# Thirty-two bytes of padding ahead of the activation and weight pools

## The chip, the cores and the metric

The kernel runs on one core of a Trainium2 chip. The metric is device microseconds of one execution; lower is better. Three runs of the kernel before took 594.8, 599.28 and 600.5 us, so the median is 599.28 us and the runs lie 1% apart.

## The reference

A decoder trunk of two layers works on 256 tokens of width 1024, in float32. Layer 0 is causal attention (one block of 256 keys, so the block selection never selects a past block), layer 1 is attention over a window of 128 keys with sinks and keys and values shared by four query heads. Behind each attention stands a gated feed-forward part with a causal convolution of width 3. Cut to the parts that take the time:

```python
x = x + o.transpose(0, 2, 1, 3).reshape(B_, S_, N_HEADS * HEAD_DIM) @ w_o
x = x + conv_ffn(rmsnorm(x, ffn_norm[l]), w_up[l], conv_w[l], conv_b[l], w_down[l])
...
def conv_ffn(h, w_up, conv_w, conv_b, w_down):     # w_up 1024 x 5632, w_down 2816 x 1024
    u = h @ w_up
    up = jnp.pad(u, ((0, 0), (CONV_W - 1, 0), (0, 0)))
    u = conv_b + sum(conv_w[j] * up[:, j:j + S_] for j in range(CONV_W))
    gate, val = jnp.split(u, 2, axis=-1)
    return (jax.nn.silu(gate) * val) @ w_down
```

## The kernel before, in words

**Products in three.** Each float32 operand is split into a high part and a low part of type fp32r, and each product is three matmuls: high by high, high by low, low by high. The weights arrive as units of 128 partitions x 2048 numbers, 1 MB each. SyncE issues their loads into three `wr` buffers, ScalarE copies a unit to its high part `wh` (line 150), VectorE subtracts to get the low part `wl` (line 153); there are four buffers of each.

**Stages.** Layer 0: projections to q, k and v (`proj`, lines 281 to 283: 512 columns of a weight unit are the moving operand, 128 tokens of an activation tile the stationary one), attention (lines 365 to 441), output projection (`Down.mm`, lines 487, 488 and 492, in the same form), up projection (lines 575 to 577: here 256 tokens of an activation tile are the moving operand and 128 columns of a weight unit the stationary one; 22 units of 48 matmuls), down projection (`Down.mm` again). Layer 1 repeats these with narrower key and value projections.

**Order.** The order of TensorE, ScalarE and VectorE is that of emission, which `tick`, `chain` and `require` set by estimated times in the program. Nothing in these estimates looks at an address.

**Where tiles lie.** SBUF is filled pool by pool, in the order in which the pools are made, and tile by tile within a pool, each at a multiple of 32 bytes:

```python
one = ctx.enter_context(tc.tile_pool(name="one", bufs=1))
qd = ctx.enter_context(tc.tile_pool(name="qd", bufs=15))
wk = ctx.enter_context(tc.tile_pool(name="wk", bufs=2))
wp = ctx.enter_context(tc.tile_pool(name="wp", bufs=4))
```

`one` holds what stays (the residual `xr`, the identity, the values `v`, the zero-padded keys `kd`, small tables), `qd` the 15 activation tiles `q` of 4096 bytes per partition, `wk` short-lived tiles (`m2`, `m3`), `wp` the buffers `wr`, `wh` and `wl` of 8192 bytes. The places within 256 bytes, as the built program has them, since sizes in `qd` and `wp` are multiples of 256 and so every buffer of a kind has the same place:

| tiles | before | after |
|---|---|---|
| `ones`; `xr` | 0; 32 | 0; 32 |
| `ident`, `v`, `kd`, `rb` | 32, 64, 192, 0 | 64, 96, 224, 32 |
| `q` (activations, high and low) | 32 | 64 |
| `m2`, `m3` | 160, 96 | 192, 128 |
| `wr`, `wh`, `wl` (weights) | 96 | 128 |

Of the kernel before, what the change touches and what calls it, by code (L numbers as in the profile page):

```python
# [7 lines left out]
F32 = mybir.dt.float32  # L8
# [6 lines left out]
P = 128  # L15
# [22 lines left out]

# columns of the packed per-partition constants
G_ATTN0, G_KV, G_ATTN1 = 0, 8, 16  # L40
# [3 lines left out]

# weight units, in the order of their use
U_V0 = 0
# [14 lines left out]
def trunk(ctx: ExitStack, tc, x, xT, pos, cpk, fin, sinks, w, out):  # L61
# [33 lines left out]

# [1 line left out]
    # Instructions are issued in the order of emission. clock is the tensor engine's progress; what waits for another  # L97
    # engine is put off by an estimated latency, behind work that is ready by then.
    clock = [0.0]
# [17 lines left out]
    def chain(key, *steps, urgent=0):  # L117
        """steps: (delay after the step before, function)."""
        def run(k):
            if urgent:  # L120
                with tc.high_priority(offset=urgent):
                    steps[k][1]()
            else:
                steps[k][1]()
            if k + 1 < len(steps):
                put_off.append((clock[0] + steps[k + 1][0], key, lambda: run(k + 1)))
        put_off.append((clock[0] + steps[0][0], key, lambda: run(0)))

    def require(*key):
        """emit now what is put off under this key."""  # L130
        while True:
            mine = [t for t in put_off if t[1] == key]
            if not mine:
                return
            run_item(min(mine, key=lambda t: t[0]))

# [1 line left out]
    wq = {}  # L138
# [20 lines left out]
    def prepare(i):  # L159
        """split the weights of unit i, paced by the tensor engine."""  # L160
        if i >= N_UNITS:
            return
        n = 4 if i <= 5 or 1 <= i - U_UP0 <= 3 or 1 <= i - U_UP1 <= 3 else 2
        cut = [slice(k * UNIT // n, (k + 1) * UNIT // n) for k in range(n)]
        w_time[0] = max(clock[0] + 200.0, w_time[0] + 4500.0)

        def first():
            weights(i)
            hi_part(i, cut[0])

        def last():
            lo_part(i, cut[-1])
            fetch(i + 3)

        steps = [(w_time[0] - clock[0], first)]
        for k in range(n - 1):
            steps.append((2000.0 / n, lambda k=k: lo_part(i, cut[k])))
            steps.append((2000.0 / n, lambda k=k: hi_part(i, cut[k + 1])))
        chain(("w", i), *steps, (2000.0 / n, last))

    def used(i):
        """all products with unit i are emitted: its place is that of unit i + 4."""
        prepare(i + 4)
# [13 lines left out]

# [1 line left out]
    ident = one.tile([P, P], F32, name="ident")  # L199
# [10 lines left out]
    def warm_up(n):  # L210
        """products that nothing reads keep the tensor engine's clock up while the first loads are under way."""
        if n:
            t = bank("u")
            for _ in range(int(n)):
                nc.tensor.matmul(t[:, :P], ones, ones, start=True, stop=True)

# [1 line left out]
    sums = {}  # L218

    def new_hT():  # L220
        """feature-major activations: hi and lo, 8 chunks of [128, 256] in two tiles each."""
        return [(quad(), quad()) for _ in range(2)]

    def feats(b, n, sets, key, keep=None):
        """half n of the residual of token block b, times gains, to feature-major hi and lo parts."""
        ts = [bank("t"), bank("t")]
        for j in range(4):
            nc.tensor.transpose(ts[j // 2][:, (j % 2) * P:(j % 2 + 1) * P],
                                xr[b][:, (4 * n + j) * P:(4 * n + j + 1) * P], ident)
        tick(450)  # L230

        def steps(hT, g, y, m):
            c = slice(2 * m, 2 * m + 2)
            hi, lo = (part[:, c, blk(b)] for part in hT[n])
            y_ = y[:, c]

            def gain():
                for j in range(2):
                    col = g + 4 * n + 2 * m + j
                    nc.scalar.activation(y_[:, j], ts[m][:, j * P:(j + 1) * P], AF.Copy, scale=cp[:, col:col + 1])  # L240

            def parts():
                nc.vector.tensor_copy(hi, y_)
                nc.vector.tensor_tensor(out=lo, in0=y_, in1=f(hi), op=ALU.subtract)

            return gain, parts

        for k, (hT, g) in enumerate(sets):
            y = mid().rearrange("p (j t) -> p j t", j=4) if keep is None else keep[n][:, :, blk(b)]
            for m in range(2):  # L250
                gain, parts = steps(hT, g, y, m)
                chain(key, (200.0 + 1000.0 * k + 500.0 * m, gain), (500.0, parts))
# [7 lines left out]
    def rstd_of(b):  # L260
        """rsqrt(mean(x^2) + eps) of the residual rows of token block b."""
        require("sq", b)
# [11 lines left out]
    def proj(o, hT, b, wv, units=()):  # L274
        """o[128 tokens of block b, n] = h @ W; wv(c) -> (hi, lo) of rows chunk c; units end with this block."""
        n = o.shape[-1]
# [28 lines left out]
    def rope(t, nh, b):  # L305
        """t: [128, nh, 64] in place."""
        ta = wk.tile([P, 8, ROT], F32, tag="ta", name=nm("ta"), bufs=1)[:, :nh]
# [10 lines left out]
    def to_feature(t, n, b, hi, lo, key, then=None):  # L318
        """t: [128 tokens, n*128] -> hi, lo [128, n, tokens of block b]."""
        pt = bank("t")  # L320
# [14 lines left out]
    def rotate(o, n, b, hi, lo, key, copy, then=None):  # L335
        """projection o of token block b: copy(t) scales it out of PSUM, then rope and transpose to hi, lo."""
        t = mid()[:, :n * P]
# [4 lines left out]
    def attention(qk, ready, filler, lead, rate, msk, vcol, sink):  # L342
        """8 pairs of heads; qk[g] = (q hi, q lo, k hi, k lo, k chunk, diagonal k); filler: products that fill the waits."""
        oT = []
# [89 lines left out]
        def values(j, pT):  # L434
            """feature-major attention of a pair of heads, and its hi and lo parts."""
            require("pT", j)
# [31 lines left out]
    class Down:  # L468
        """residual += parts^T @ W, rows of 1024; two K chunks a unit; wait(i): parts of unit i are emitted."""

# [32 lines left out]
        def finish(self, i0, after, tail=None):  # L503
            """units from i0, so ordered that half of a token block is ready after each step."""
            last = self.n_u - 1
# [21 lines left out]
        def end(self, b, n, tail):  # L527
            """the last unit's products with one half of the columns, in two pieces of their own."""
            i = self.n_u - 1
# [26 lines left out]
    def ffn(layer, u_up, u_dn, hT, y, rb, after, tail=None):  # L556
        parts = []
# [22 lines left out]
        def scale_x(m):  # L580
            """chunks 2m and 2m + 1 of the activations times rstd, in parts, for the units from n_raw."""
            c = slice(2 * (m % 2), 2 * (m % 2) + 2)
# [73 lines left out]
    def row_bcast(rb, b):  # L656
        """rb[:, block b] = 1 / rms of each token, on all partitions."""
        r = rstd_of(b)
# [14 lines left out]

# [1 line left out]
    hT = new_hT()  # L675
# [50 lines left out]

    # rotary tables: cs = [cos cos], sn = [-sin sin] per token
    invf = one.tile([P, HALF], F32, name="invf")
# [84 lines left out]
    def spread(g, src, w):  # L813
        """keys of block 0 of two chunks to the diagonal: the heads of a pair side by side."""
        for e in range(2):
# [19 lines left out]
    qk = {}  # L835
# [69 lines left out]

# [1 line left out]
    kT = quad()  # L907
# [66 lines left out]
    def tail(m, o):  # L974
        """the last quarter rows of token block 1: residual, sum of squares, and after the last one the scaled rows."""
        st = sums[1]
# [31 lines left out]
def pack(inp):  # L1008
    """Weights as [unit, 128, 2048] in the order of use, rows of K on the partitions."""
    import numpy as np  # L1010
# [29 lines left out]
    halves(k_major(inp["w_kv_b"]))  # L1040
    # the heads of a pair belong to neighbouring key heads
    order = [(2 * (j // 4) + e) * 4 + j % 4 for j in range(NH // 2) for e in range(2)]
# [46 lines left out]
```

## Time and profile before

| what | value |
|---|---|
| runs, us | 594.8, 599.28, 600.5 |
| profiled execution | span 594.0 us; the page gives no time of its own beside the span |
| TensorE busy | 583.7 us of the span |
| VectorE busy | 430.1 us |
| ScalarE busy | 382.4 us |
| GpSimd busy | 106.0 us |
| DMA | 45.4% of 16 engines' span, 101 MB |
| granted TensorE clock | 0.999, mean over the span |

A matmul's busy time in the records overlaps with that of the next, because matmuls are pipelined. What a matmul costs in a dense stream is read from the distance between the starts of neighbours, not from its own duration. Over a long stretch that distance is the time from the first start to the last, divided by the number of matmuls between.

### The profile page before, as it was taken

The page shows a single profiled execution, that of the slowest core. Times are in us where ns is not written, and L with a number is a line of the kernel's source. Part 1 is how long each engine was busy: PE and PEld are TensorE (multiplying, and loading weights), DVE is VectorE, ACT ScalarE, POOL GpSimd, SP SyncE. Part 2 cuts the span into 40 slices and gives each one's busy share as a digit, 9 for nine tenths or more (in the row PEclk, how much of TensorE's full clock was granted, in tenths as well). Part 3 has the DMA queues.
Part 4 walks back from the last instruction along what each step waited for, and adds up shares of the span by engine and source line. Part 5 has one row for each costly group of instructions (what it writes and reads, how often), then busy time and mean ns, then how long its engine had stood idle before and what let it go on. Part 6 is the DMA issues. An engine that isn't in the chain of part 4 may idle for free.

```text
span 594.0 us, 10194 instructions
## 1 busy us (share of the span) xinstructions
PE 583.7 (98%) x3858; PEld 513.4 (86%) x3858; DVE 430.1 (72%) x927; ACT 382.4 (64%) x769; POOL 106.0 (18%) x124
## 2 busy tenths in 40 slices
PE   7999999999999999999999999999999999999995
PEld 6877777789999999988878977679999999988884
DVE  4597668589977777776369778769987677777714
ACT  5788767578566565656349688757865565656513
POOL 6321101001222323220001100000222223232003
PEclk9999999999999999999999999999999999999999
DMA  7963534314554444548542622233273545445701
GB/s 237 394 247 128 213 142 142 142 38 177 213 189 167 182 173 163 193 151 333 191 175 83 273 72 72 72 142 137 90 271 143 204 151 189 168 168 222 284 0 71
DMA packets 17184, 101.00 MB, mean 170 GB/s; under 512 B 2288, under 2 KB 2672, under 8 KB 5744
## 3 DMA queue, kind: packets, MB, share of 16 engines
q1 hardware_dynamic: 16992, 100.09, 45.4%
q8 instruction: 30, 0.49, 0.3%
q10 hardware_dynamic: 144, 0.26, 0.1%
q14 instruction: 18, 0.15, 0.1%
HBM read 99.30 MB, written 1.05 MB: 169 GB/s over the span
## 4 chain that ended last, share of the span: by engine, by line
PE 72%; DVE 9%; ACT 7%; POOL 4%; issue 4%; DMA 2%; SPq 0%; POOLq 0%; DVEq 0%; ACTq 0%
PE acc L487 9%; PE acc L488 9%; PE acc L492 9%; POOL m L619 4%; PE acc L281 4%; PE acc L282 4%; PE acc L283 4%; PE u L575 4%; PE u L576 3%; PE u L577 3%; PE t L575 3%; PE t L576 3%; PE t L577 3%; PE t L441 3%; DVE wl L153 2%
## 5 line engine op out<-in xcount | busy, mean ns | idle before, releaser
L153 DVE TENSOR_TENSOR wl<-wr,wh 128x1024 fp32r<-128x1024 f32 (+1 forms) x208 | 224.7, 1100 | 42.2 <-ACT wh L150 41.8
L150 ACT ACTIVATE wh<-wr 128x1024 fp32r<-128x1024 f32 (+1 forms) x208 | 192.7, 956 | 41.8 <-PE acc L492 26.9
L619 POOL TENSOR_TENSOR m<-m,m 128x256 f32<-128x256 f32 x44 | 67.1, 1527 | 205.9 <-DVE m L614 177.6
L487 PE MATMUL acc<-wh,q 128*128 128x512 f32 x238 | 96.2, 404 | 0.0
L488 PE MATMUL acc<-wl,q 128*128 128x512 f32 x238 | 94.8, 398 | 0.0
L575 PE MATMUL u<-q,wh 128*128 128x256 f32 x320 | 89.5, 281 | 0.0
L576 PE MATMUL u<-q,wh 128*128 128x256 f32 x320 | 89.1, 279 | 0.0
L577 PE MATMUL u<-q,wl 128*128 128x256 f32 x320 | 89.1, 279 | 0.0
L575 PE MATMUL t<-q,wh 128*128 128x256 f32 x288 | 80.4, 279 | 0.2 <-DVE m L614 0.2
L492 PE MATMUL acc<-wh,q 128*128 128x512 f32 x238 | 80.4, 399 | 0.0
L577 PE MATMUL t<-q,wl 128*128 128x256 f32 x288 | 80.3, 279 | 0.0
L576 PE MATMUL t<-q,wh 128*128 128x256 f32 x288 | 80.3, 279 | 0.0
L623 ACT ACTIVATE q<-m 128x256 fp32r<-128x256 f32 x44 | 18.4, 417 | 82.0 <-POOL m L619 82.0
L575 PEld LDWEIGHTS u<-q,wh 128*128 128x128 f32 x320 | 60.5, 190 | 0.1
L577 PEld LDWEIGHTS u<-q,wl 128*128 128x128 f32 x320 | 60.2, 188 | 0.0
L576 PEld LDWEIGHTS u<-q,wh 128*128 128x128 f32 x320 | 60.1, 188 | 0.0
L281 PE MATMUL acc<-wh,q 128*128 128x512 f32 (+1 forms) x160 | 57.7, 361 | 0.0
L282 PE MATMUL acc<-wl,q 128*128 128x512 f32 (+1 forms) x160 | 56.4, 353 | 0.1
L283 PE MATMUL acc<-wh,q 128*128 128x512 f32 (+1 forms) x160 | 56.2, 351 | 0.0
L575 PEld LDWEIGHTS t<-q,wh 128*128 128x128 f32 x288 | 54.7, 190 | 0.3 <-issue 0.3
L576 PEld LDWEIGHTS t<-q,wh 128*128 128x128 f32 x288 | 54.1, 188 | 0.0
L577 PEld LDWEIGHTS t<-q,wl 128*128 128x128 f32 x288 | 54.1, 188 | 0.0
(150 smaller groups left out, 1029.3 us busy)
## 6 DMA issues: line engine op xcount, KB each, us to landing
wr<-in_w SPq DMA_DIRECT2D x89, 1024.0 KB, 4.8
wr<-in_w SPq DMA_DIRECT2D x12, 256.0 KB, 5.6
xr<-in_x SPq DMA_DIRECT2D x4, 256.0 KB, 7.4
x<-in_xT SPq DMA_DIRECT2D x3, 256.0 KB, 6.2
out<-m SPq DMA_DIRECT2D x3, 256.0 KB, 2.3
fin_t<-in_fin SPq DMA_DIRECT2D x1, 512.0 KB, 5.7
x<-in_xT SPq DMA_DIRECT2D x2, 128.0 KB, 2.7
out<-m ACTq DMA_DIRECT2D x1, 256.0 KB, 2.0
```

Source lines behind the costliest of these rows:

```text
L150: nc.scalar.activation(wq[i][0][:, c], raws[i][:, c], AF.Copy)
L153: nc.vector.tensor_tensor(out=wq[i][1][:, c], in0=raws[i][:, c], in1=f(wq[i][0][:, c]), op=ALU.subtract)
L281: nc.tensor.matmul(o, xh[:, blk(b)], wh, start=(c == 0), stop=False)
L282: nc.tensor.matmul(o, xh[:, blk(b)], wl, start=False, stop=False)
L283: nc.tensor.matmul(o, xl[:, blk(b)], wh, start=False, stop=(c == KC - 1))
L487: nc.tensor.matmul(o, ph[:, blk(b)], hi[:, s_], start=first, stop=False)
L488: nc.tensor.matmul(o, ph[:, blk(b)], lo[:, s_], start=False, stop=False)
L492: nc.tensor.matmul(o, pl[:, blk(b)], hi[:, s_], start=False, stop=end)
L575: nc.tensor.matmul(o, hi[:, s_], xh, start=(c == 0), stop=False)
L576: nc.tensor.matmul(o, hi[:, s_], xl, start=False, stop=False)
L577: nc.tensor.matmul(o, lo[:, s_], xh, start=False, stop=(c == KC - 1))
L619: nc.gpsimd.tensor_tensor(out=h, in0=gs, in1=t[1], op=ALU.mult)
```

## The change

One tile of 8 float32 numbers per partition, 32 bytes, is reserved in pool `one` behind `xr` and never used. All that is reserved after it lies 32 bytes further on. Beside that the comments and docstrings are taken out. Every engine's instructions, their order, shapes and waits stay as they were; only addresses differ.

```diff
     nc.scalar.activation(warm, warm, AF.Sin)
     xr = [one.tile([P, D], F32, name=f"xr{b}") for b in range(NB)]
 
-    # ---- constants ---------------------------------------------------------
+    one.tile([P, 8], F32, name="pad")
+
+
     ident = one.tile([P, P], F32, name="ident")
```

## Rows read from the trace of the kernel before

**Rows 1.** The page: span, and busy time of each engine.

```profile
span 594.0 us, 10194 instructions
PE 583.7 (98%) x3858; PEld 513.4 (86%) x3858; DVE 430.1 (72%) x927; ACT 382.4 (64%) x769; POOL 106.0 (18%) x124
```

**Rows 2.** Busy time by stretch: us, engines' busy us (instructions), clock, DMA share, GB/s.

```profile
138.00:251.00 113.00, 113.00 (x962) 113.00 (x961) 87.81 (x144) 70.98 (x118) 28.85 (x19) 1.00 0.47 176
251.00:303.00 52.00, 52.00 (x226) 42.16 (x225) 30.98 (x37) 25.98 (x33) 4.68 (x3) 1.00 0.60 221
...
412.00:514.40 102.40, 102.40 (x906) 102.40 (x905) 81.95 (x135) 66.29 (x107) 24.24 (x16) 1.00 0.48 181
...
525.00:581.00 56.00, 56.00 (x247) 45.59 (x246) 31.44 (x39) 25.01 (x33) 6.23 (x4) 1.00 0.43 160
```

**Rows 3.** Line 575, 150 to 245 us: count, duration min/median/max, first and last start.

```profile
L575 PE MATMUL u<-q,wh x142: 281/281/281, 149.7 to 244.8; 128*128 128x256 f32 x142
...
L575 PE MATMUL t<-q,wh x128: 281/281/281, 155.0 to 239.5; 128*128 128x256 f32 x128
```

**Rows 4.** Line 575, 430 to 510 us.

```profile
L575 PE MATMUL u<-q,wh x121: 276/276/276, 429.8 to 508.6; 128*128 128x256 f32 x121
...
L575 PE MATMUL t<-q,wh x116: 276/276/276, 432.8 to 510.0; 128*128 128x256 f32 x116
```

**Rows 5.** Line 487, 256 to 300 us, then 530 to 580 us.

```profile
L487 PE MATMUL acc<-wh,q x63: 397/397/398, 255.8 to 299.2; 128*128 128x512 f32 x63
...
L487 PE MATMUL acc<-wh,q x71: 397/397/398, 530.4 to 579.4; 128*128 128x512 f32 x71
```

**Rows 6.** Timeline of TensorE, first projections: start, duration, line (lines 282, 283 left out).

```profile
26.20 0.39 PE L281 MATMUL acc<-wh,q 128*128 128x512 f32 x1
...
26.88 0.39 PE L281 MATMUL acc<-wh,q 128*128 128x512 f32 x1
...
27.57 0.39 PE L281 MATMUL acc<-wh,q 128*128 128x512 f32 x1
```

**Rows 7.** Timeline of TensorE at two interruptions of the up projection.

```profile
132.20 0.28 PE L577 MATMUL acc<-q,wl 128*128 128x256 f32 x1
132.32 0.38 PE L663 MATMUL t<-m,ones 128*128 128x128 f32 x2
132.46 0.36 PE L575 MATMUL u<-q,wh 128*128 128x256 f32 x1
...
514.19 0.28 PE L576 MATMUL t<-q,wh 128*128 128x256 f32 x1
514.30 0.28 PE L577 MATMUL t<-q,wl 128*128 128x256 f32 x1
514.42 0.33 PE L575 MATMUL u<-q,wh 128*128 128x256 f32 x1
514.58 0.28 PE L576 MATMUL u<-q,wh 128*128 128x256 f32 x1
514.70 0.28 PE L577 MATMUL u<-q,wl 128*128 128x256 f32 x1
```

**Rows 8.** Timeline of TensorE: scores, with the tile `kd` as moving operand.

```profile
339.64 0.28 PE L365 MATMUL u<-kd,q 128*128 128x256 f32 x1
339.76 0.28 PE L366 MATMUL u<-kd,q 128*128 128x256 f32 x1
339.88 0.28 PE L367 MATMUL u<-kd,q 128*128 128x256 f32 x1
```

**Rows 9.** Groups by line and shape: count, busy us, mean ns, idle before.

```profile
L487 PE MATMUL acc<-wh,q 128*128 128x512 f32 x238 | 96.2, 404 | 0.0
...
L281 PE MATMUL acc<-wh,q 128*128 128x512 f32 x96 | 38.9, 405 | 0.0
...
L839 ACT ACTIVATE m<-acc,rstd 128x512 f32<-128x512 f32 x8 | 5.3, 679 | 0.9 <-PE acc L283 0.9
...
L720 ACT ACTIVATE v<-acc,rstd 128x512 f32<-128x512 f32 x4 | 2.7, 684 | 1.2 <-PE acc L283 0.7 <-POOL rstd L267 0.5
```

## The prediction

> **What bounds the kernel.** I read the busy times first. TensorE is busy 583.7 of 594.0 us, VectorE 430.1, ScalarE 382.4 [rows 1]. So 10.3 us at most can come from filling TensorE's gaps, and any larger gain or loss has to come from how fast TensorE gets through its own matmuls. Next I cut the span into stages [rows 2]. In the long ones TensorE is busy the whole time: 113.00 of 113.00 us in the up projection of layer 0, 52.00 of 52.00 in the down projection behind it, and the same in layer 1. VectorE, the next engine, has 87.81 of 113.00 and 81.95 of 102.40 us, and DMA is at 0.43 to 0.60. None of them sets the pace there, and the granted clock is 1.00 throughout, the 2.4 GHz level.
>
> Third, the pace of the matmuls themselves, from first and last starts. In layer 0's up projection line 575 runs 142 + 128 = 270 times from 149.7 to 244.8 us [rows 3]. Each is one of three (lines 575 to 577), so 269 x 3 = 807 matmuls take 95.1 us: **117.8 ns** from start to start. In layer 1 it is 121 + 116 = 237 times from 429.8 to 510.0 us [rows 4], 236 x 3 = 708 matmuls in 80.2 us: **113.3 ns**. It is the same code with the same shapes, and its tiles have the same places within 256 bytes. The down projections, 512 columns, go at (299.2 - 255.8) / (62 x 3) = **233.3 ns** and (579.4 - 530.4) / (70 x 3) = 233.3 ns [rows 5]. The first projections, also 512 columns, go at (27.57 - 26.20) / 6 = **228.3 ns** [rows 6].
>
> So there are at least two paces, 4.5 ns apart at 256 columns and 5.0 ns at 512. What switches between them is seen at two places [rows 7]. At 514.30 to 514.42 us the pace is still the short one; the matmul at 514.42 starts the next one only 0.16 us later, and from there on the starts are 0.12 us apart, with the same activation tiles. At 132.32 us two matmuls of another shape come in between, and the stream that follows is that of [rows 3]. The pace is thus a pattern into which the stream of weight loads and moving reads falls, and an interruption of some 0.05 to 0.1 us throws it anew. The places of the tiles within 256 bytes did not choose it here, since they are the same in both layers.
>
> **The profiled execution against the runs.** The page has no time for it beside the span. The fastest run, 594.8 us, is 0.8 us above the span, and I take 0.8 us as what lies around: 594.8 us of its own. The median of the three runs, 599.28, is 4.5 us above that. If the 906 instructions of layer 1's up projection [rows 2] had gone at the long pace, they would have taken 906 x 4.5 ns = 4.1 us more. That is nearly all of the difference, so I read the runs as two throws: one execution of three with layer 1 at the short pace, two with it at the long one.
>
> **The change, part by part.** It removes no instruction, adds none and moves none, on any queue; the reserved 32 bytes are never written. The comments cost nothing, since they are not part of the program. What is left is addresses.
>
> *ScalarE, VectorE, GpSimd.* The nearest row for a place that is a multiple of 64: ScalarE writes 128 x 512 from PSUM to `v` (place 64) in 684 ns and to `m2` (place 160) in 679 ns [rows 9]. The 5 ns are within what such rows scatter, so I cost these engines at 0. What hides them is TensorE, busy all the time; if the cover were gone, 0.7% of VectorE's 430.1 us would be 3 us at most, in either direction.
>
> *DMA.* Weight buffers start at 96 before and at 128 after, and DMA is at most 0.60 busy in the dense stages [rows 2]. I cost it at 0.
>
> *TensorE.* Both operands move by the same 32 bytes, so their places relative to each other stay as they were (64 apart). Only their places against larger blocks change: activations and weights began 32 past a multiple of 64, and now begin on one. The trace has no such stream. The nearest row is the scores, whose moving operand `kd` begins at 192, a multiple of 64, with the stationary `q` at 32: its starts are 0.12 us apart [rows 8], the long pace of 256 columns and no better. So an aligned moving operand alone gains nothing; an aligned stationary one beside it is not shown. I take 0, by this nearest row, and bound the cost as follows.
>
> Upwards and downwards within the two paces seen: all at the short pace takes 962 x 4.5 ns = 4.3 us from layer 0's up projection and (226 + 247) x 5.0 ns = 2.4 us from the down projections [rows 2], 6.7 us in all: 588.1 us. All at the long pace adds 4.1 us and, for the other matmuls of 512 columns, (3 x 238 + 3 x 96 - 473) x 5.0 ns = 2.6 us [rows 2, 9]: 601.5 us. Outside them, one more step of the same size in every matmul: the 2 x 22 x 48 = 2112 of the up projections by 4.5 ns and the 1002 of 512 columns [rows 9] by 5.0 ns, 14.5 us. That is 588.1 - 14.5 = 573.6 us at the one end and 601.5 + 14.5 = 616 us at the other.
>
> The rows say that the same matmul has two paces [rows 3, 4]. The Trainium skill says otherwise (SBUF — State Buffer, section Who interferes with whom): TensorE has two read ports of its own, one for the moving operand and one for weight loads, and never waits on anyone. By that rule no place in SBUF could matter and the sum would be 0 as well, but there would be one pace, and the trace does not agree. The skill (TensorE: Matmul & The Clock Gate, section Back-to-back issue gap) puts the warm gap at N / 2.4 + 2.5 ns, 109.2 and 215.8 ns, which no run here shows; worked out from it as an estimate, a stream at those gaps would end some 22 us below the case with the short pace everywhere, at 566 us.
>
> **Sum:** 594.8 + 0, with the pace of layer 1's up projection left to the throw: 594.8 if short, 598.9 if long, against runs of 594.8 to 600.5. I forecast the middle of the fastest run and the median, **597 us**.
>
> **The rivals.**
>
> *A, the forecast (0.48): the paces stay, the throw is as before.* For it: same instructions, same relative places, and two paces at the same addresses [rows 3, 4]. 594 to 601 us.
>
> *B (0.22): the new places make the short pace the one the streams fall into.* For it: the pace is set by how two reads fall against each other, and their starts against blocks of 64 bytes do change. Against it: [rows 8]. 588 us.
>
> *C (0.14): whole blocks make a pace shorter than any seen,* because each read of 1024 or 2048 bytes touches one block less. For it: the paces at 256 and 512 columns differ by 115 ns, so nearly all of a matmul's time goes with the bytes that it reads. Against it: [rows 8] again, and that nothing like it shows. About 573 us.
>
> *D (0.14), the other side: both reads now begin on a block's edge and collide.* The weight load for the next matmul runs beside the moving read; if the two now ask for the same part at once, the pattern can be a step longer than the long pace. It would decide from 117.8 ns in layer 1's up projection on: at one step all over, 616 us; in the up projections alone, 601.5 + 9.5 = 611 us.
>
> *E (0.02): the edit does nothing,* because an unused tile gets no room. The built addresses say that it gets it. 597 us.
>
> **How the numbers follow.** About 1%, 6 us, is what can be told from no change here: 593.3 to 605.3 around the median. Faster is B and C, 0.36. Same is A and E, 0.50. Slower is D, 0.14. The range from 572 to 604 takes in A, B, most of C and the mild part of D; left out are the far ends of C and D, some 0.18. The forecast's own range is 594 to 601.
>
> **What would show it.** The starts of lines 575 to 577 in both up projections, and of lines 487 to 492 in the down projections. A: 113.3 and 117.8, 228 and 233 ns, in another mixture. B: 113.3 in both layers and 228 in the down projections. C: below 113 and 228. D: above 117.8 or 233.3. In all cases VectorE's and ScalarE's rows by shape stay within 1 to 2%. The forecast is wrong if a pace appears that is in no row here, or if both layers settle at the same short pace in each run.

## The result and the profile after

The changed kernel takes **591.34 us** in the median of 20 runs (589.71 to 594.97), the kernel before 595.53 us in the median of 20 (591.48 to 600.5). The ratio is **0.9935**, interval 0.9912 to 0.9958: faster by 0.65%. The profiled execution took 593.47 us with a span of 591.5 us, so 2.0 us lie around the span; the ratio is taken over the runs and is not the quotient of the two medians. The runs of before fall into three groups: 4 at 591.5 to 592.6, 10 at 594.5 to 596.2, 6 at 598.8 to 600.5. Of the changed kernel's, 16 lie below 592.2 and 4 at 593 to 595. The profiled execution is one of those 4, and 2.4 us above the middle of the other 16, 591.06 us; of these 16 there is no trace.

The page first, as in [rows 1].

```profile
span 591.5 us, 10194 instructions
## 1 busy us (share of the span) xinstructions
PE 579.9 (98%) x3858; PEld 508.6 (86%) x3858; DVE 430.4 (73%) x927; ACT 383.5 (65%) x769; POOL 106.1 (18%) x124
```

VectorE, ScalarE and GpSimd are busy as long as before, within 1.1 us. TensorE has 3.8 us less with the same 3858 instructions, so the same matmuls went by faster. By stretch, columns as in [rows 2]:

```profile
139.00:236.70 97.70, 97.70 (x864) 97.70 (x863) 77.23 (x127) 62.24 (x101) 24.22 (x16) 1.00 0.49 173
...
411.00:513.00 102.00, 102.00 (x901) 101.98 (x900) 81.27 (x132) 65.25 (x106) 25.43 (x17) 1.00 0.51 176
...
523.00:579.00 56.00, 56.00 (x245) 45.49 (x244) 31.45 (x40) 24.45 (x33) 6.23 (x4) 1.00 0.43 160
```

In layer 0's up projection 864 instructions pass in 97.70 us; before it was 962 in 113.00 [rows 2], and 864 at that pace would be 101.5. The lines of the kernel are numbered two higher now, so line 577 answers to 575 in [rows 3, 4], first for 141 to 235 us and then for 428 to 508 us:

```profile
L577 PE MATMUL u<-q,wh x128: 276/276/276, 149.7 to 230.9; 128*128 128x256 f32 x128
...
L577 PE MATMUL t<-q,wh x123: 276/276/276, 155.1 to 234.7; 128*128 128x256 f32 x123
...
L577 PE MATMUL u<-q,wh x119: 276/276/276, 427.8 to 506.0; 128*128 128x256 f32 x119
...
L577 PE MATMUL t<-q,wh x117: 276/276/276, 430.2 to 507.7; 128*128 128x256 f32 x117
```

Layer 0: 250 x 3 = 750 matmuls from 149.7 to 234.7 us, 113.3 ns each, where [rows 3] gave 117.8. Layer 1: 235 x 3 = 705 in 79.9 us, 113.3 ns, as in [rows 4]. The down projection, line 489 for 487 in [rows 5], 256 to 290 us:

```profile
L489 PE MATMUL acc<-wh,q x49: 397/397/398, 255.9 to 289.5; 128*128 128x512 f32 x49
```

33.6 us / (48 x 3) = 233.3 ns, unchanged. Laid side by side by number of matmul, the two traces lose and gain in few places: 0.8 us lost in the first projections, up to 45 us; 0.1 us lost in the 6 us ahead of line 665 below; 4.0 us gained from 133 to 237 us; 0.4 us lost at 242 us, where TensorE waits at the end of layer 0's up projection. From there on stages differ by hundredths of a us. Together that is the 2.6 us between the two spans. The loss in the first projections need not be the change's: against the kernel before, the traces of the kernels in the next section lie between 0.3 us earlier and 0.6 us later there.

The place where layer 0's pace is thrown is that of the first three rows of [rows 7]. TensorE's timeline of the changed kernel there, with the weight load (PEld) of line 665 beside it:

```profile
133.00 0.28 PE L578 MATMUL acc<-q,wh 128*128 128x256 f32 x1
133.12 0.28 PE L579 MATMUL acc<-q,wl 128*128 128x256 f32 x1
133.12 0.31 PEld L665 LDWEIGHTS t<-m,ones 128*128 128x128 f32 x2
133.24 0.38 PE L665 MATMUL t<-m,ones 128*128 128x128 f32 x2
133.38 0.37 PE L577 MATMUL u<-q,wh 128*128 128x256 f32 x1
133.58 0.28 PE L578 MATMUL u<-q,wh 128*128 128x256 f32 x1
133.70 0.28 PE L579 MATMUL u<-q,wl 128*128 128x256 f32 x1
133.82 0.28 PE L577 MATMUL u<-q,wh 128*128 128x256 f32 x1
133.93 0.28 PE L578 MATMUL u<-q,wh 128*128 128x256 f32 x1
134.04 0.28 PE L579 MATMUL u<-q,wl 128*128 128x256 f32 x1
```

Ahead of line 665 starts are 0.12 us apart, behind it they settle at 0.11. In the kernel before it was the other way round, 0.11 ahead of it

```profile
131.75 0.28 PE L576 MATMUL acc<-q,wh 128*128 128x256 f32 x1
131.86 0.28 PE L577 MATMUL acc<-q,wl 128*128 128x256 f32 x1
131.97 0.28 PE L575 MATMUL acc<-q,wh 128*128 128x256 f32 x1
```

and 0.12 behind it. This short matmul, which spreads 1/rms over the partitions, reads the tile `ones` as weights and a short tile `m3` as moving operand.

### The profile page after: what moved, and what is told of

It reads as the page before. It is cut to its first block, busy times and chain, and to the rows that moved or that the text cites. A ratio compares the mean times of both kernels' runs of the same rounds, so it can differ in the third digit from the quotient of the medians.

```text
span 591.5 us, 10194 instructions
## 1 busy us (share of the span) xinstructions
PE 579.9 (98%) x3858; PEld 508.6 (86%) x3858; DVE 430.4 (73%) x927; ACT 383.5 (65%) x769; POOL 106.1 (18%) x124
## 4 chain that ended last, share of the span: by engine, by line
PE 54%; DVE 15%; ACT 10%; POOL 8%; issue 6%; DMA 3%; SPq 1%; POOLq 0%; DVEq 0%; ACTq 0%
PE acc L489 9%; PE acc L490 9%; PE acc L494 9%; POOL m L621 8%; DVE m L616 5%; DVE m L614 5%; DVE wl L153 4%; ACT m L610 4%; PE acc L283 4%; PE acc L284 4%; PE acc L285 4%; DMA wr<-in_w 3%; PE t L443 3%; ACT q L625 2%; PE t L422 2%
## 5 line engine op out<-in xcount | busy, mean ns | idle before, releaser
L577 PE MATMUL t<-q,wh 128*128 128x256 f32 x288 | 79.8, 277 | 0.5 <-DVE m L616 0.5
```

What stands on the lines that cost most here:

```text
L577: nc.tensor.matmul(o, hi[:, s_], xh, start=(c == 0), stop=False)
```

## The experiments

The kernel before ran beside each set again; as its runs fall into groups, its median there was 599.0, 596.08 and 598.9 us, and the ratios' intervals carry that. Below, "distance" is the start of the weights minus the start of the moving operand within 256 bytes, so that 192 and -64 are the same.

Three theories stood at first: that reads which begin on a multiple of 64 bytes take the short pace more often (block64), that the throw does not look at addresses at all, and that the traffic of the other engines makes the long pace (neighbours).

**Streams alone.** Two kernels leave the decoder out and run nothing but streams of one matmul, each behind a short interrupting one of another length:

```diff
+    for a in range(4):          # moving operand at 0, 32, 64, 96 within 256 bytes
+        for b in range(4):      # weights at 64, 96, 128, 160
+            for n in range(8):  # eight interrupters
+                ...
+                for k in range(36):
+                    nc.tensor.matmul(acc[n % 2][:, :256], st[b][:, :P], mv[a][:, :256], start=(k == 0), stop=(k == 35))
```

> A stream alone: the decoder is left out, and TensorE runs matmuls of 256 columns, 128 streams of 36, with nothing beside them on the other engines. The moving operand starts at 0, 32, 64 or 96 within 256 bytes, the weights at 64, 96, 128 or 160, each pair in eight streams that begin behind an interrupting matmul of another length. Theory block64 (a read that starts on a multiple of 64 bytes falls into the short pace more often): pairs with both starts on a multiple of 64 run at 113.3 ns in most of their eight streams, pairs with both 32 past one at 117.8 ns in most. Theory throw (only the moment at which a stream begins picks the pace): both paces, 113.3 and 117.8 ns, appear in every pair, in the same share. Theory neighbours (the other engines' traffic makes the long pace): a stream that runs alone has one pace only, 113.3 ns or less, in all pairs.

Measured, from the timeline of TensorE; 36 matmuls stand in one row, whose second column is the time from the first start to the last end:

```profile
78.99 4.51 PE L97 MATMUL acc<-mova,statc 128*128 128x256 f32 x36
...
184.70 4.34 PE L97 MATMUL acc<-movb,statb 128*128 128x256 f32 x36
188.88 0.17 PE L95 MATMUL u<-mova,stata 128*128 128x16 f32 x1
...
193.11 4.49 PE L97 MATMUL acc<-movb,statb 128*128 128x256 f32 x36
...
289.12 4.56 PE L97 MATMUL acc<-movc,stata 128*128 128x256 f32 x36
...
359.71 4.35 PE L97 MATMUL acc<-movc,statc 128*128 128x256 f32 x36
...
363.92 4.49 PE L97 MATMUL acc<-movc,statc 128*128 128x256 f32 x36
```

`movb` with `statb` is the pair of places of the kernel before (32 and 96), `movc` with `statc` that of the changed kernel (64 and 128). Both have both paces: 4.34 and 4.49 us a row, which from the seventh start to the last is 113.3 and 117.8 ns a matmul. Each has the short one in 5 of its 8 streams; `mova` with `stata` and `movd` with `statd`, the other two pairs at distance 64, have it in 3 and in 2. So **block64 falls**, and so does the theory of neighbours, since no other engine works here. The throw theory holds only in part: the short pace appears in no other pairs than the four whose distance from moving operand to weights is 64. `mova` with `statc` (distance 128) goes at 118.7 ns, `movc` with `stata` (distance 0) at 120.

> The same stream alone with 512 columns, 128 streams of 24. Block64: pairs with both starts on a multiple of 64 run nearer to 226 to 229 ns, pairs 32 past one at 233.3 ns. Throw: the same mixture of 228 to 229 and 233.3 ns in every pair. Neighbours: one pace, 229 ns or less, everywhere.

The same with 512 columns gave 226.6 to 227.4 ns at distance 0, whatever the places, and 232 to 234.5 ns at all other distances from -32 to 160. None of the theories had foreseen that either.

**Other shifts.** The edit is the size of the reserved tile:

```diff
-    one.tile([P, 8], F32, name="pad")
+    one.tile([P, 16], F32, name="pad")     # pad64; 24 in pad96
```

> The reserved tile has 64 bytes instead of 32: activations at 96 and weights at 160 within 256 bytes, both 32 past a multiple of 64 as in the kernel before. Block64: as before, 592 to 600 us with about a fifth of the runs below 593, ratio 0.998 to 1.002 to the kernel before. Throw by the mere fact of a shift: anything between 590 and 599 us, unrelated to the place.

> The reserved tile has 96 bytes: activations at 128 and weights at 192 within 256 bytes, both on a multiple of 64 as in the changed kernel. Block64: as the changed kernel, about 591 us in most runs, ratio 0.991 to 0.996. Throw: anything between 590 and 599 us, and no closer to the changed kernel than the run with 64 bytes.

`pad64` took 593.19 us (ratio 0.992, 0.9884 to 0.9955): 5 runs of 10 at 590.3 to 591.7, 5 at 594.7 to 596.1. `pad96` took 590.6 us (0.9884, 0.9846 to 0.9922), all six runs below 591.7. So a shift that leaves both reads 32 past a multiple of 64 gained too, in half of its runs as much as the change: block64 falls here too. In `pad96` the down projections had become faster as well. Its line 489 from 251 to 290 us:

```profile
L489 PE MATMUL acc<-wh,q x57: 388/388/394, 251.3 to 289.7; 128*128 128x512 f32 x57
```

38.4 us / (56 x 3) = 228.6 ns instead of 233.3. In the trace of `pad64` the down projection of layer 0 still goes at 233 ns and that of layer 1 at 229.

**A new theory: distances.** The pace hangs on the distance between the two reads, not on where they lie; the change leaves that distance alone for the long streams, and alters others: that of the identity to the residual, and that of `ones`, which does not move, to the tiles that do. Four runs tell this from a theory of places. First the paces by distance, moving operand fixed at 0:

```diff
+    for size in (256, 512):
+        for b in range(8):      # weights at 0, 32, ... 224 within 256 bytes
+            for n in range(8):
+                ...
+                    nc.tensor.matmul(acc[n % 2][:, :size], st[b][:, :P], mv[:, :size], start=(k == 0), stop=(k == 29))
```

> The decoder is left out; one moving operand at 0 within 256 bytes, weights at 0, 32, ... 224, streams of 30 matmuls of 256 and then of 512 columns, eight per pair. The two earlier stream runs covered distances (weights minus moving operand) of -32 to 160. Theory relative (the pace hangs on the distance between the two reads within 256 bytes and not on where either lies): distance 64 gives 113.3 and 117.8 ns again, 0 gives 120 and 226.6 ns, 32 gives 118.3 ns, 96 gives 117 to 120 ns, 128 gives 118.7 and 232.8 ns, 160 gives 120 ns, 224 gives 116.6 to 117.9 ns; 192, which the projections have, gives the 228 to 229 and 233.3 ns of the kernel. Theory place: the paces differ from those by 1 ns or more, since the moving operand now always begins on a multiple of 256.

Three streams of the timeline at distance 64, then one at distance 0 and one at 192 with 512 columns:

```profile
67.19 3.78 PE L96 MATMUL acc<-mov,statc 128*128 128x256 f32 x30
70.81 0.17 PE L94 MATMUL u<-mov,stata 128*128 128x16 f32 x1
70.84 3.67 PE L96 MATMUL acc<-mov,statc 128*128 128x256 f32 x30
...
74.37 3.78 PE L96 MATMUL acc<-mov,statc 128*128 128x256 f32 x30
...
256.59 7.09 PE L96 MATMUL acc<-mov,stata 128*128 128x512 f32 x30
...
583.23 7.12 PE L96 MATMUL acc<-mov,statg 128*128 128x512 f32 x30
```

All eight distances, ns per matmul from a stream's seventh start to its last, over eight streams:

| weights minus moving operand | 256 columns | 512 columns |
|---|---|---|
| 0 | 119.7 to 120.0 | 226.7 to 227.2 |
| 32 | 118.2 to 118.4 | 233.2 to 233.4 |
| 64 | 113.3 (5 streams), 117.7 to 117.8 (3) | 233.3 to 233.4 |
| 96 | 117.2 to 118.5 | 234.3 |
| 128 | 118.5 to 118.8 | 232.1 to 233.5 |
| 160 | 119.8 to 120.2 | 233.4 |
| 192 | 117.7 to 117.8 | 228.7 to 229.0 |
| 224 | 116.6 to 117.7 | 233.3 |

Every distance repeats the paces that it had at other places, most of them to 0.5 ns; at 96 and 128 single streams of 256 columns had reached 120.0 in the earlier run. The theory of places falls. Distance 64 with 256 columns has two paces 4.5 ns apart. It is not alone in having two: in these runs streams of one pair differ by 1 ns or more at 96, 128 and 224 too, as the table and the earlier run show, by up to 2.8 ns.

Second, everything moved together:

```diff
+    one.tile([P, 8], F32, name="pad")
     cp = one.tile([P, NCOL], F32, name="cp")
```

> The 32 bytes are reserved ahead of the first tile of all, so every tile moves by 32 bytes, the ones and the residual too: activations at 64 and weights at 128 as in the changed kernel, and every distance between two tiles as in the kernel before. Theory relative, with the throw made by the distances that the change does alter (identity to residual, ones to short tiles): the kernel before again, ratio 0.998 to 1.002, most runs at 595.5 and 599, few below 593. Theory place (the new places themselves): the changed kernel, ratio 0.990 to 0.996, most runs at 591.

It took 599.23 us, ratio **1.0002** (0.9966 to 1.0037): 8 runs of 12 at 598.9 to 600.2, one below 594. Activations and weights lie where the change puts them, and nothing is gained. Its line 577, 430 to 510 us, layer 1:

```profile
L577 PE MATMUL u<-q,wh x115: 281/281/281, 429.9 to 509.7; 128*128 128x256 f32 x115
...
L577 PE MATMUL t<-q,wh x112: 281/281/281, 433.4 to 506.5; 128*128 128x256 f32 x112
```

79.8 us / (226 x 3) = 117.7 ns: the long pace, in layer 1 too.

Third, identity, values, zero-padded keys and `rb` moved alone:

```diff
     r_t = one.tile([P, 1], F32, name="r_t")
+    one.tile([P, 56], F32, name="back")     # beside the 8 numbers of the change
```

> 32 bytes behind the residual and 224 bytes at the end of the same pool: identity, values, zero-padded keys and rb move by 32 bytes as in the changed kernel, activations, short tiles and weights lie as before. Theory relative: the transposes of the residual, whose distance to the identity is changed as in the changed kernel, throw the streams behind them, so times move towards the changed kernel, ratio 0.990 to 0.997. If only activations and weights count: the kernel before, ratio 0.998 to 1.002.

599.09 us, ratio 1.002 (0.9994 to 1.0045): the kernel before. My guess that the transposes throw the pace was a miss, and what is left is the distance of `ones` to the tiles that moved behind it.

Fourth, the long streams' own distance changed, from 64 to 32:

```diff
     wp = ctx.enter_context(tc.tile_pool(name="wp", bufs=4))
     ps = ...
+    wk.tile([P, 56], F32, name="back", bufs=1)     # beside the 8 numbers of the change
```

> As the changed kernel up to the activations, and the rest 32 bytes back: activations at 64, weights at 96, so the distance from moving operand to weights is 32 instead of 64 in the up projections. Theory relative: up projections at 118.3 ns in both layers with no short pace, and projections of 512 columns at 233.2: 599 to 602 us in every run, ratio 1.000 to 1.008. Theory place: activations on a multiple of 64 give half of the gain, 592 to 597 us.

601.69 us, ratio 1.0077 (1.0049 to 1.0106), all nine runs within 601.2 to 602.5. Line 578 from 430 to 510 us:

```profile
L578 PE MATMUL u<-q,wh x114: 277/281/285, 430.0 to 509.9; 128*128 128x256 f32 x114
...
L578 PE MATMUL t<-q,wh x112: 277/280/285, 435.0 to 508.4; 128*128 128x256 f32 x112
```

79.9 us / (225 x 3) = 118.4 ns, the pace of distance 32 alone. The paces of the bare streams carry over, and with distance 32 the groups are gone.

**The interrupter alone.** One tile moved, everything else at the places of before:

```diff
+    one.tile([P, 56], F32, name="pad")
     ones = one.tile([P, P], F32, name="ones")
+    one.tile([P, 8], F32, name="back")
```

> The kernel before with one tile moved alone: the ones lie at 224 within 256 bytes instead of 0, everything else at the places of before. The short matmul that interrupts each up projection reads the ones as weights and a short tile (96) as moving operand; its distance is now 224 - 96 = 128, which is 0 - 128 in the changed kernel, and was 160 before. Theory interrupter (this distance throws the pace of the long stream behind it): the changed kernel's times though activations and weights lie as before, most runs 589 to 592 us, ratio 0.987 to 0.996. If it counts for nothing: the kernel before, groups at 592, 595.5 and 599, ratio 0.998 to 1.002.

591.34 us, ratio **0.9907** (0.9871 to 0.9943), 9 runs of 10 at 590.5 to 592.1. Line 578 of it from 140 to 235 us:

```profile
L578 PE MATMUL u<-q,wh x128: 276/276/276, 148.5 to 229.7; 128*128 128x256 f32 x128
...
L578 PE MATMUL t<-q,wh x127: 276/276/276, 153.9 to 234.8; 128*128 128x256 f32 x127
```

86.3 us / (254 x 3) = 113.3 ns in layer 0. Nothing but the first warming matmuls reads `ones` beside the interrupter. Giving `ones` the distance to the other tiles that it has in the changed kernel gives its time, with activations and weights where they were. That, and the nothing of `shift_all`, settle which consequence of the change counted.

They do not settle which partner of `ones` counts. The expectation names the interrupter's own moving operand `m3`: 160 before, 128 in the changed kernel and here. But the weight load of `ones` is recorded beside the matmul ahead, whose moving operand is `q` (133.12 us in the timeline above), and that distance goes from 224 to 192 in both kernels as well. `q` and `m3` lie 64 apart wherever the long streams keep their distance of 64, so no run here separates the two. The distances below are those to `m3`.

The interrupter of this kernel:

```profile
131.80 0.28 PE L579 MATMUL acc<-q,wh 128*128 128x256 f32 x1
131.91 0.28 PE L580 MATMUL acc<-q,wl 128*128 128x256 f32 x1
132.03 0.38 PE L666 MATMUL t<-m,ones 128*128 128x128 f32 x2
132.17 0.37 PE L578 MATMUL u<-q,wh 128*128 128x256 f32 x1
...
132.83 0.28 PE L580 MATMUL u<-q,wl 128*128 128x256 f32 x1
132.95 0.28 PE L578 MATMUL u<-q,wh 128*128 128x256 f32 x1
133.06 0.28 PE L579 MATMUL u<-q,wh 128*128 128x256 f32 x1
```

Here the pace is 0.11 us ahead and 0.11 behind, where the kernel before went from 0.11 to 0.12. The same reading in both layers of every trace whose long streams have distance 64 gives:

| distance of `ones` to `m3` | traces | pace ahead of the interrupter, and behind it |
|---|---|---|
| 160 | before, `shift_all`, `one_only` | short to long 5 times, long to short once |
| 128 | after, `ones_224` | short to short twice, long to short twice |
| 96 | `pad64` | short to short twice |
| 64 | `pad96`, `two_places` | short to short once, long to short 3 times |

So the interrupter was no fair throw at any of these places. At 160 it turned the pace over each time; at the others the stream behind it had the short pace each time, whatever came ahead. As far as six layers show, what differs from execution to execution at 160 would then be the pace ahead of it.

**A better version.** From the table: distance 64 for the up projections, 0 for matmuls of 512 columns. On top of `pad96`, activation tiles that serve as stationary operand begin 64 bytes into a longer buffer:

```diff
-    def quad():
-        return qd.tile([P, 4, S], F32R, tag="q", name=nm("q"))
+    def quad(off=0):
+        t = qd.tile([P, 4 * S + 64], F32R, tag="q", name=nm("q"))
+        return t[:, off:off + 4 * S].rearrange("p (a s) -> p a s", a=4)
...
-                pq = quad()
+                pq = quad(16)     # likewise the other stationary ones
```

> As the run with 96 reserved bytes, and activation tiles that serve as stationary operand beside moving weights begin 64 bytes into a longer buffer, at 192 as the weights do; those that are the moving operand stay at 128. Distances: 64 in the up projections as ever, 0 instead of 192 in projections and down projections. By the paces of the streams alone, 1002 matmuls of 512 columns go at 226.7 instead of 228.9 to 233.3 ns: 2 us less than the run with 96 bytes, 587 to 589 us, ratio 0.980 to 0.988 to the kernel before, with lines 487 to 492 at 226.7 ns in both layers. If the paces of the streams alone do not carry over into the kernel: 590 to 592 us.

**588.87 us**, ratio 0.987 (0.9821 to 0.9919), six runs at 588.2 to 590.2: the fastest of all by its median. Its interval overlaps with that of `pad96`, so that it beats `pad96` is shown by the pace below and not by the time. Line 490 from 526 to 566 us:

```profile
L490 PE MATMUL acc<-wh,q x59: 389/389/389, 525.7 to 565.2; 128*128 128x512 f32 x59
```

39.5 us / (58 x 3) = 227 ns, where the changed kernel has 233.3 and `pad96` 228.6.

## Why the prediction was right or wrong

*What bounds the kernel:* right. All that moved is TensorE's pace in streams that fill it wholly; the other engines' busy times stayed within 1.1 us.

*Two paces, chosen by an interruption:* right, and it was the key. The 113.3, 117.8, 228 and 233.3 ns of A are the paces of the changed kernel's stages too. C and D, a pace beyond them, did not come. The Trainium skill (SBUF — State Buffer, section Who interferes with whom) has TensorE's two read ports as independent. The pace here is not independent of how the two reads lie: with nothing else running, their distance alone took 256 columns from 113.3 to 120.2 ns.

*"The places of the tiles within 256 bytes did not choose it here":* this step failed. It was argued from two layers with the same places and different paces. That shows a throw, not that the throw is fair. The interrupter has a distance of its own, and it loads the throw. By their times most runs at 160 (before, `shift_all`, `one_only`) have a long layer, and most at 128 (the change, `ones_224`) have none.

*"Both operands move by the same 32 bytes":* right for the long streams, and I took it for the whole of TensorE. The same table of places showed `ones` at 0 before and after and `m3` at 96 and then 128; I did not follow these two into the matmul of line 663, which stands in [rows 7].

*The sum.* A's "throw as before" failed, and the median lies below A's own 594 to 601; it lies in the wide range because B is in there. What came in the profiled execution is the first term of B alone. It had put 4.3 us on 962 matmuls of layer 0 at the short pace; measured 4.0 us, since a hold-up of 0.07 us at 236.7 us ended the short pace before the projection's end. B's second term, 2.4 us from the down projections, did not come there: 233.3 ns stayed, as that stage began behind a long-paced end. The 16 shorter runs are 2.4 us shorter in the middle; whether that is this term, no trace shows. Both up projections at the short pace was my own sign that the forecast is wrong, and the profiled execution has it, though "in each run" is not shown. The estimate from the Trainium skill's warm gap (TensorE: Matmul & The Clock Gate, section Back-to-back issue gap) comes to 21 us, 2112 x 4.1 ns and 1002 x 12.5 ns, and not 22; besides, that section gives the gap for a matmul by itself and not for a stream of weight loads and matmuls.

*0.8 us around the span:* too little, by the changed kernel's 2.0 us. The profiled execution of before then took some 596.0 us, a run of the middle group.

*One execution of three with a short layer, two with none:* right in kind. Twenty runs show three groups 3.6 us or so apart, which fits no layer, one layer and both layers at the long pace. The traces of before (one layer long, some 596.0 us) and of `shift_all` and `one_only` (both long, 599.42 and 598.96 us) bear that out. The median of three, 599.28, happened to be of the slowest group; over twenty it is 595.53. So of the 5.7 us between my 597 and 591.34, 1.5 us are that base and 4.2 us the change, which my parts put at 0; that 597 lay 2.3 us below the median that I had came from choosing a point between it and the fastest run. "Within 1%" holds.

*Still open:* what in the chip ties the pace to the distance; why the down projections can run at 233.3 ns in the kernel at distance 192, which the bare stream never did (they did so behind an up projection that ended at the long pace, and at 228.6 in `pad96` behind one that ended at the short); whether `ones` counts by its distance to `m3` or to `q`; and how that distance acts. The bare streams did not vary the places of the interrupting pair, so whole kernels alone show it: beside the traces above, no run of 6 at 64 (`pad96`) has the time of a long layer, and 5 of 10 at 96 (`pad64`) have, though of these 5 there is no trace.

## What to carry to other kernels

Where TensorE is busy all the time, read its pace from starts and look whether one shape has two; then ask what stands just ahead of the stream. When addresses move, list which pairs of operands keep their distance and which do not, short matmuls included, before saying that nothing changed. A tile's place is a free knob: here moving one buffer of ones was worth the whole change (ratio 0.9907 beside 0.9935), and with distances chosen per stage as well the ratio is 0.987, of which `pad96` has 0.9884 without that choice.

## What the runs showed of the hardware that I had not expected

The distance within 256 bytes between the moving read and the weight load sets the pace of fp32r matmuls: 113.3 to 120.2 ns at 256 columns, 226.6 to 234.5 ns at 512, on an otherwise idle core. The best distance is not the same for both shapes: 0 is among the slowest for 256 columns and the fastest for 512. At distance 64 a stream of 256 columns has two lasting paces, 113.3 and 117.8 ns, and one interrupting matmul of 0.14 us decides for some 100 us, worth 4.0 us in layer 0. Where its weights lie against the tiles around it decides how: in one place it turned the pace over, 6 times of 6, in three others it led to the short pace, 10 times of 10. The Trainium skill's warm gap (TensorE: Matmul & The Clock Gate, section Back-to-back issue gap), 109.2 and 215.8 ns for a matmul by itself, was reached in these streams at no distance; the measured floor here is 113.3 and 226.6.
